# Attention's last two heads issued inside the first column group of the output projection, and the residual rows loaded behind that group

## The chip, the cores and the metric

The kernel runs on one core of a Trainium2 chip. A core has a matrix engine (PE, TensorE), a vector engine (DVE), a scalar engine (ACT), a general engine (POOL, hardly used here) and SP, which issues the transfers between device memory and the core's own memory. Each engine works through its own queue in order and waits for the others by semaphores. The metric is the time of one execution in microseconds of device time, the median of several runs.

## What is computed

A two-layer trunk on one sequence of 512 tokens with 2048 features, all in float32. Layer one is an mLSTM; layer two, which the change touches, is a chunked band attention over 16 heads of 128 features with a gate, then an output projection, a normalisation, and the residual. Cut to that:

```python
def band_attention_mixer(h, k, v, w_in, rel_table, w_out):
    Bn, S, _ = h.shape
    qz = h @ w_in
    q = qz[..., :B_WIDTH].reshape(Bn, S, B_HEADS, B_DH)
    z = qz[..., B_WIDTH:]
    o = chunk_band_attention(q, k, v, rel_table)
    y = o.reshape(Bn, S, B_WIDTH) * jax.nn.silu(z.astype(F32))
    return y.astype(h.dtype) @ w_out
...
        x = (x.astype(F32) + gate[:, None, :] * rmsnorm(y, g_post[l])).astype(x.dtype)
```

`chunk_band_attention` scales the scores of a head's queries with its keys, adds a bias by relative position, masks what lies ahead of the chunk, takes a softmax over the keys, and multiplies with the values. k and v come from one shared projection (kv_w) computed before.

## The kernel before, in words

**Precision.** Every product of float32 numbers is made of three matmuls: each operand is split into a high part (a cast on ACT, line 181) and a low part (a subtraction on DVE, line 182), and high x high, high x low and low x high are summed. All matmuls are issued from line 223 (`mm`), the transposes from line 1014.

**Weights.** They stream in as pieces of up to 128 x 1024 numbers (512 KB), in one fixed order. `wpiece` (its load is line 199) takes the next piece: it loads it into a raw buffer (`wr`), casts the high part (`wh`) and subtracts the low part (`wl`). Raw buffers rotate; every third piece can go to an own buffer in a pool named by `spare`, where one is set. Pieces are issued ahead of the work that uses them by a scheduler with priorities, as far as buffers are free. The same raw buffers take the rows `y2r` that are mentioned below.

**Attention.** For each head h, `queries(h, mid)` projects queries and gate (`proj_s`, tiles ps_dz, ps_cz, ps_az, ps_bz, four pieces of weights a head), scales the queries, takes the gate's SiLU (`sz`), splits the keys and fetches the bias (line 983). `weights(h, ...)` makes four rounds of scores (`ps_s`), adds the bias and takes the row's extreme (line 1001), exponentiates on ACT (line 1002), and normalises on DVE (lines 1003 and 1004). `flipped(h, ...)` transposes the weights (`ps_t`, ten transposes, line 1014), splits them (`pt`) and the values (`vv`). `mixed(h, ...)` multiplies them with the values (`ps_o`), multiplies with the gate on DVE (line 1032) and stores the product in device memory (`y2c`, line 1033). Keys and values of a head come from device memory by `fetch` (lines 961 and 962), three heads at a time. The steps are staggered: while head h's query projection runs, its third piece's hook (`mid`) issues `mixed(h-2)` and `weights(h-1)`, and `flipped(h-1)` follows the projection. After head 15's projection two rounds are left, without a projection beside them: `mixed(14)`, `weights(15)`, `flipped(15)`, and then `mixed(15)`.

**The last output projection.** It has four column groups of 512 columns (g). In a group, `proj_b` goes through eight pieces of weights, two blocks of 128 rows each (k0 = 0, 2, ... 14), with four sums `ps_y` open (one for each 128 tokens, m): 24 matmuls a piece, 192 a group. The left operand is read back from `y2c`, two heads at a time, by `y2_tile` (`y2r`, line 1071) and split into `y`; it is kept for the other groups. `proj_b` takes a table `at` of hooks by k0, which are called ahead of the piece. At a group's end each sum is evicted (`evac`, line 782) and squared (line 783). The fourth group is done in two halves, and the finished rows get the norm and the residual (`finish`) between and behind them. The residual rows `x2` (eight loads of 512 KB, line 1062) are issued ahead of the first group.

**Memory.** Pools are opened and closed like a stack, on a left and a right side; a new pool's tiles lie over those of closed ones and wait for their last readers. `kq` (operands of the query projection, and before the change the key and value rows), and `att` (the rest of attention) are on the left and close together at attention's end; `op` (the evicted sums) and `x2` are opened over them.

Of the kernel before, what the change touches and what calls it, by code (L numbers as in the profile page):

```python
# [9 lines left out]
F32 = mybir.dt.float32  # L10
# [5 lines left out]
P = 128  # L16
D = 2048
S = 512
KT = D // P
# [8 lines left out]
BH = 16  # L28
# [7 lines left out]
PAIRS = [(0, 1), (2, 3)]  # L36
# [96 lines left out]
def hybrid_trunk(ctx, tc, xT, xN, c, adaT, cols, wst, wg, ext, kc, out):  # L133
    nc = tc.nc
# [8 lines left out]
    def pool(name, bufs=1, **kw):  # L143
        return tc.tile_pool(name=name, bufs=bufs, reuse_waits="tile", **kw)
# [5 lines left out]
    xsc = dram.tile([4, P, D], F32, name="xsc")  # L150
# [34 lines left out]
    spare = [None]  # L185
# [58 lines left out]
    def proj_b(mat, xs, pss, ms=range(4), kts=KT, at={}, late=0):  # L244


        held = []
        for k0 in range(0, kts, 2):
            if k0 in at:
                at[k0]()  # L250
            held.append((k0, *wpiece(mat)[0]))
            if k0 >= kts - 2 * late and k0 < kts - 2:
                continue
            for group in [[pm] for pm in zip(pss, ms)] if k0 == kts - 2 else [list(zip(pss, ms))]:
                for ka, hi, lo in held:
                    for j in range(2):
                        k = ka + j
                        x = xs(k) if callable(xs) else xs[k]
                        w = slice(j * 512, (j + 1) * 512)
                        for ps, m in group:  # L260
                            t = slice(m * P, (m + 1) * P)
                            mm3(ps, x[:, 0, t], x[:, 1, t], hi[:, w], lo[:, w], k == 0, k == kts - 1)
            held.clear()
# [136 lines left out]
    for q in range(4):  # L400
        t = sp.tile([P, 4, S], F32, name=f"xt{q}")
# [8 lines left out]
    for i in range(4):  # L410
        ps = newp(f"ps_c{i}")
# [8 lines left out]
    for q in range(4):  # L420
        pair = []
# [30 lines left out]
    for k0, k1 in BLOCKS:  # L452
# [10 lines left out]
        for i, acc in enumerate(later):  # L463
            ps = newa(f"ps_l{i}_{k0}")
# [154 lines left out]
    for h in range(NH):  # L619
# [6 lines left out]
        for i in range(4):  # L626
            if h > HALF:
                if i % 2 == 0:
                    zs = pair((i // 2) * (V0 // 2) + h * DK, f"zq{h}_{i}")
                ps = zs[i % 2]  # L630
            elif h < 2:
                ps = (lead, qk1)[h][i]
            else:
                ps = newp(f"ps_qk{h}_{i}")
# [24 lines left out]
        pr, tot = [], []  # L659
        at = {8 + 2 * j: lambda j=j: scores(h, j, qk, pr, nm, nmd, tot) for j in range(4)} if h else {}  # L660
# [11 lines left out]
        for m in range(4):  # L672
            if m < 3:
                t = hp.tile([P, 2, S], F32R, tag="qk", name=f"v{h}_{m}", bufs=4)
                split(t[:, 0, :], t[:, 1, :], pv[m])
            else:
                t = hp.tile([P, S], F32, tag="v3", name=f"v{h}_{m}")
# [6 lines left out]
        for i in range(4):  # L684
            if h >= HALF:
                f = HEAD_PAIRS if h > HALF else RAMP[i]
# [5 lines left out]
            elif h:  # L692
                ps = newp(f"ps_o{h}_{i}")
# [87 lines left out]
    def evac(ps, m, g, dst):  # L781
        nc.vector.tensor_tensor(dst, ps, gb, op=ALU.mult)
        nc.scalar.activation(newa(f"sqy{m}_{g}"), ps, AF.Square, accum_out=ssq[:, 4 * m + g : 4 * m + g + 1])
# [169 lines left out]
    tst.close()  # L953


    at = ast.enter_context(pool("att"))
    kv = []

    def fetch(h):
        t = kq.tile([P, 2, S], F32, tag="kv", name=f"kv{h}", bufs=3)  # L960
        nc.sync.dma_start(t[:, 0, :], ksc[h // 2][:, h % 2, :])
        nc.sync.dma_start(t[:, 1, :], vsc[h // 4][:, h % 4, :])
        kv.append(t)
# [3 lines left out]
    def queries(h, mid):  # L967

        if h < BH - 1:
            fetch(h + 1)  # L970
        z = at.tile([P, 4, 256], F32, tag="z", name=f"z{h}", bufs=2)
        proj_s("b_w_in", h2, h2s, ATT_PAIRS, z[:, 0:2, :], z[:, 2:4, :], f"z{h}", kq, 3, {2: mid})
        qz = z.rearrange("p a t -> p (a t)")
        nc.scalar.mul(qz[:, :S], qz[:, :S], P**-0.5)
        q = at.tile([P, 2, 384], F32R, tag="q", name=f"q{h}", bufs=2)
        split(q[:, 0, :], q[:, 1, :], qz[:, P:S])
        sz = qz[:, S:]
        nc.scalar.activation(sz, sz, AF.Silu)
        k = at.tile([P, 2, S], F32R, tag="kk", name=f"k{h}")
        split(k[:, 0, :], k[:, 1, :], kv[h][:, 0, :])  # L980
        bias = at.tile([P, S], F32, tag="b", name=f"bias{h}", bufs=2)
        b0 = bsc[h]
        nc.sync.dma_start(bias, bass.AP(b0.tensor, b0.offset + P - 1, [[EXTW - 1, P], [1, S]]))
        nc.vector.memset(bias[:64, 448:512], NEG)
        return (qz[:, :P], q, k, bias), sz

    def weights(h, q0, q, k, bias):

        mx = at.tile([P, 12], F32, tag="mx", name=f"mx{h}", bufs=2)
        pr = []  # L990
        for i in range(4):
            n = P * (i + 1)
            ps = newa(f"ps_s{h}_{i}")
            if i == 0:
                mm(ps[:, :n], q0, kv[h][:, 0, :P], True, True)
            else:
                t = slice(P * (i - 1), P * i)
                mm3(ps[:, :n], q[:, 0, t], q[:, 1, t], k[:, 0, :n], k[:, 1, :n], True, True)
            s = at.tile([P, n], F32, tag=f"s{i}", name=f"s{h}_{i}")
            m, l, r = (mx[:, 3 * i + j : 3 * i + j + 1] for j in range(3))  # L1000
            nc.vector.tensor_tensor_reduce(s, ps[:, :n], bias[:, S - n :], -1.0, 3e38, ALU.add, ALU.min, m)
            nc.scalar.activation(s, s, AF.Exp, bias=m, scale=-1.0, accum_out=l)
            nc.vector.reciprocal(r, l)
            nc.vector.tensor_scalar(s, s, r, None, op0=ALU.mult)
            pr.append(s)
        return pr

    def flipped(h, pr):
        pts = []
        for j in range(4):  # L1010
            n = S - P * j
            ps = newa(f"ps_t{h}_{j}")
            for i in range(j, 4):
                nc.tensor.transpose(ps[:, P * (i - j) : P * (i - j + 1)], pr[i][:, P * j : P * (j + 1)], ident)
            if j < 3:
                t = at.tile([P, 2, n], F32R, tag=f"pt{j}", name=f"pt{h}_{j}")
                split(t[:, 0, :], t[:, 1, :], ps[:, :n])
            else:
                t = at.tile([P, n], F32, tag=f"pt{j}", name=f"pt{h}_{j}")
                nc.scalar.copy(t, ps[:, :n])  # L1020
            pts.append(t)
        v = at.tile([P, 2, 384], F32R, tag="vv", name=f"vv{h}")
        split(v[:, 0, :], v[:, 1, :], kv[h][:, 1, :384])
        return pts, v

    def mixed(h, pts, v, sz):
        ps = newa(f"ps_o{h}")
        for j in range(3):
            d = slice(P * j, P * (j + 1))
            mm3(ps[:, P * j :], v[:, 0, d], v[:, 1, d], pts[j][:, 0, :], pts[j][:, 1, :], j == 0, False)  # L1030
        mm(ps[:, 384:], kv[h][:, 1, 384:], pts[3], False, True)
        nc.vector.tensor_tensor(sz, ps, sz, op=ALU.mult)
        nc.sync.dma_start(y2c[h // 2][:, h % 2, :], sz)

    qs, ptv, szs = {}, {}, {}
    for h in range(BH + 2):
        pr = []

        def mid():
            if h > 1:  # L1040
                mixed(h - 2, *ptv.pop(h - 2), szs.pop(h - 2))
            if 0 < h <= BH:
                pr.extend(weights(h - 1, *qs.pop(h - 1)))

        if h < BH:
            qs[h], szs[h] = queries(h, mid)
        else:
            mid()
        if 0 < h <= BH:
            ptv[h - 1] = flipped(h - 1, pr)  # L1050
    ast.close()


    ost = ExitStack()
    op = ost.enter_context(pool("op", bufs=KT))
    rp = spare[0] = ost.enter_context(pool("x2", bufs=8))
    yo = [[] for _ in range(4)]
    x2 = []
    for m in range(4):
        t = [rp.tile([P, 2, S], F32, tag="x2", name=f"x2_{m}_{i}") for i in range(2)]  # L1060
        for i in range(2):
            nc.sync.dma_start(t[i], xsc[m, :, 2 * i * S : 2 * (i + 1) * S].rearrange("p (a t) -> p a t", a=2))
        x2.append([t[g // 2][:, g % 2, :] for g in range(4)])

    y2 = []

# [11 lines left out]
    def finish(m):  # L1078
        rs = row_rstd(m)
        for g in range(4):  # L1080
            y = yo[m][g]
            nc.vector.scalar_tensor_tensor(y, y, rs, x2[m][g], op0=ALU.mult, op1=ALU.add)
            nc.sync.dma_start(out[m, :, g * S : (g + 1) * S], y)

    for g in range(4):
        gate_row(1, g)
        for pair in [range(4)] if g < 3 else PAIRS:
            ps = [newp(f"ps_y1_{g}_{m}") for m in pair]
            at = {4: lambda: finish(0), 6: lambda: finish(1)} if pair == PAIRS[1] else {}
            proj_b("b_w_out", y2_tile, ps, ms=pair, at=at, late=3 if pair == PAIRS[1] else 0)  # L1090
            with tc.high_priority(AHEAD):
                for p, m in zip(ps, pair):
                    yo[m].append(op.tile([P, S], F32, tag="o", name=f"yo{m}_{g}"))
                    evac(p, m, g, yo[m][g])
    finish(2)
    finish(3)
    assert wpos[0] == len(order)
# [56 lines left out]
```

## Time and profile before

| | |
|---|---|
| median of 3 runs | 2856.14 us (2855.57 to 2857.32) |
| span of the profiled execution | 2852.6 us, from its first to its last instruction |
| the profiled execution's own time | not measured apart from its span |
| granted PE clock, mean | 0.993 |
| attention's first query projection begins on PE | 2236.45 us |
| its last one ends on PE | 2637.06 us |
| first ps_y of the last output projection | 2659.41 us |
| first eviction of its column groups 0, 1, 2 | 2709.25, 2752.77, 2796.29 us |

The page's times are microseconds from the start of the span. A row of a timeline is start, duration, engine, line, operation, out<-in and count, and in brackets the idle time before it with what ended it; consecutive equal instructions are one row. A row of the waits is engine and line, what it waited for, the total, how often, and the longest. SPq rows are issues of transfers on SP: their duration is that of the issue and not of the transfer. In a window's row, PEclk is the granted clock as a share of full speed.

### The profile page before, as it was taken

What the parts mean: (1) busy time and instruction counts of PE and PEld (TensorE: products, weight loads), DVE (VectorE), ACT (ScalarE), POOL (GpSimd) and SP (SyncE); (2) the same over time, 40 slices, a digit from 0 to 9 for tenths busy, and PEclk for the clock granted to TensorE, in tenths of its full rate; (3) what the DMA queues carried; (4) which work ended last, traced back from release to release, by engine and by line L of the source; (5) the groups of instructions that cost most, each with busy time, mean ns of one, the idle gap of its engine ahead of it and who ended that gap; (6) DMA issues with size and microseconds to landing.
All of it is one profiled execution on the core that took longest, in us unless ns stands there. A gap on an engine that the chain in (4) does not pass through costs nothing.

```text
span 2852.6 us, 40697 instructions
## 1 busy us (share of the span) xinstructions
PE 2796.1 (98%) x15308; PEld 2425.8 (85%) x15308; DVE 2074.9 (73%) x3680; ACT 1337.4 (47%) x2005; POOL 0.2 (0%) x4
## 2 busy tenths in 40 slices
PE   7999999999999999999999999999999999999798
PEld 5787888888888989989898888888998999999687
DVE  7986978778688766857766445567875899998425
ACT  4244524234234544545545445577334566666323
POOL 0000000000000000000000000000000000000000
PEclk9999999999999999999999999999999999999899
DMA  8875687878764232332325657787336433333534
GB/s 298 301 245 185 232 308 247 296 236 279 260 236 132 93 115 97 108 100 100 104 96 168 205 197 241 232 285 259 137 137 210 141 126 117 121 126 123 184 104 173
DMA packets 177117, 524.61 MB, mean 184 GB/s; under 512 B 18788, under 2 KB 36228, under 8 KB 176408
## 3 DMA queue, kind: packets, MB, share of 16 engines
q1 hardware_dynamic: 176920, 522.01, 54.1%
q8 instruction: 120, 1.97, 0.3%
q14 instruction: 77, 0.63, 0.1%
HBM read 488.33 MB, written 38.85 MB: 185 GB/s over the span
## 4 chain that ended last, share of the span: by engine, by line
PE 86%; DVE 6%; DMA 4%; ACT 2%; issue 1%; SPq 0%; DVEq 0%; ACTq 0%
PE ps_y L223 18%; PE ps_v L223 10%; PE ps_o L223 5%; PE ps_z L223 5%; PE ps_azo L223 4%; PE ps_qk L223 4%; PE ps_kv L223 4%; PE ps_bzo L223 3%; PE ps_az L223 3%; PE ps_l L223 3%; PE ps_cz L223 2%; PE ps_dz L223 2%; PE ps_czo L223 2%; PE ps_dzo L223 2%; PE ps_s L223 2%; PE ps_bz L223 2%
## 5 line engine op out<-in xcount | busy, mean ns | idle before, releaser
L181 ACT CAST wh<-wr 128x1024 fp32r<-128x1024 f32 (+3 forms) x586 | 585.1, 1000 | 860.0 <-PE ps_y L223 210.0
L182 DVE TENSOR_TENSOR wl<-wr,wh 128x1024 fp32r<-128x1024 f32 (+3 forms) x586 | 678.5, 1160 | 421.5 <-ACT wh L181 416.7
L223 PE MATMUL ps_y<-wh,y 128*128 128x512 f32 x1536 | 478.6, 392 | 10.6 <-ACT wh L181 6.0
L223 PEld LDWEIGHTS ps_y<-wh,y 128*128 128x128 f32 x1536 | 289.9, 189 | 72.1 <-ACT wh L181 6.2
L223 PE MATMUL ps_v<-wh,h 128*128 128x512 f32 x1024 | 321.6, 390 | 0.4 <-DVE cv L529 0.4
L223 PE MATMUL ps_y<-wl,y 128*128 128x512 f32 x768 | 300.6, 391 | 0.0
L181 ACT CAST wsh<-ws 128x384 fp32r<-128x384 f32 (+1 forms) x253 | 138.4, 547 | 321.5 <-issue 127.3
L223 PEld LDWEIGHTS ps_v<-wh,h 128*128 128x128 f32 x1024 | 192.3, 188 | 40.5 <-issue 1.2
L182 DVE TENSOR_TENSOR wsl<-ws,wsh 128x384 fp32r<-128x384 f32 (+1 forms) x253 | 151.5, 599 | 99.8 <-ACT wsh L181 98.3
L223 PE MATMUL ps_v<-wl,h 128*128 128x512 f32 x512 | 199.8, 390 | 0.0
L381 DVE CUSTOM_DVE_ANT_0 ada<-ada,scB,cl 128x1024 f32<-128x1024 f32 x128 | 163.7, 1280 | 25.7 <-DMA ada<-in_adaT 25.6
L381 DVE CUSTOM_DVE_ANT_0 ada<-ada,scB,mod 128x1024 f32<-128x1024 f32 x128 | 163.9, 1280 | 19.9 <-DMA ada<-in_adaT 18.4
L223 PEld LDWEIGHTS ps_y<-wl,y 128*128 128x128 f32 x768 | 145.0, 189 | 30.6 <-DVE wl L182 0.9
L223 PE MATMUL ps_kv<-wh,hkv 128*128 128x512 f32 x512 | 159.3, 391 | 0.0
L206 DVE TENSOR_TENSOR ws<-wr 128x256 f32<-128x256 f32 (+1 forms) x253 | 112.2, 451 | 34.9 <-DMA wr<-in_wst 31.8
L223 PE MATMUL ps_qk<-h,wh 128*128 128x512 f32 x384 | 119.2, 390 | 0.0
L223 PE MATMUL ps_o<-h,wh 128*128 128x512 f32 x384 | 118.2, 389 | 0.0
L223 PE MATMUL ps_z<-h,wh 128*128 128x512 f32 x384 | 118.2, 389 | 0.0
L223 PEld LDWEIGHTS ps_v<-wl,h 128*128 128x128 f32 x512 | 96.2, 188 | 19.8 <-issue 0.9
L223 PEld LDWEIGHTS ps_kv<-wh,hkv 128*128 128x128 f32 x512 | 95.7, 188 | 19.5
L223 PE MATMUL ps_l<-h,wh 128*128 128x512 f32 x320 | 99.4, 392 | 1.3 <-ACT q L467 0.5
L223 PE MATMUL ps_kv<-wl,hkv 128*128 128x512 f32 x256 | 99.9, 390 | 0.1
(385 smaller groups left out, 5916.0 us busy)
## 6 DMA issues: line engine op xcount, KB each, us to landing
wr<-in_wst SPq DMA_DIRECT2D x520, 512.0 KB, 3.7
ada<-in_adaT SPq DMA_DIRECT2D x256, 512.0 KB, 5.9
xt<-nsc SPq DMA_DIRECT2D x46, 256.0 KB, 4.3
yr<-ysc SPq DMA_DIRECT2D x16, 512.0 KB, 4.3
wr<-in_wst SPq DMA_DIRECT2D x30, 256.0 KB, 4.0
wr<-in_wst SPq DMA_DIRECT2D x16, 384.0 KB, 5.8
bsc<-in_ext SPq DMA_DIRECT2D x16, 320.0 KB, 6.2
xt<-in_xT SPq DMA_DIRECT2D x4, 1024.0 KB, 7.0
```

The costliest lines, as they stand in the source:

```text
L181: nc.scalar.copy(hi, src)
L182: nc.vector.tensor_tensor(lo, src, hi.bitcast(F32), op=ALU.subtract)
L206: nc.vector.tensor_tensor(t[:, : 2 * w], r[:, w : 3 * w], r[:, : 2 * w], op=ALU.subtract)
L223: nc.tensor.matmul(ps, a, b, start=start, stop=stop)
L381: pin(nc.vector.tensor_tensor_reduce(at, at, scB[:, j * D // 2 : (j + 1) * D // 2], 1.0, mod[:, i : i + 1] if j else col(CB + i), ALU.mult ...
```

## The change

Three things are done. First, the last two rounds of attention are no longer issued behind head 15's projection but as hooks of the first column group of the output projection: `mixed(14)` and `weights(15)` ahead of k0 = 2, `flipped(15)` ahead of k0 = 6, `mixed(15)` ahead of k0 = 8. Second, `x2` is opened, and its eight loads are issued, behind the first column group (`last_rows`); the own raw buffer of every third piece moves to the pool `op`, which is now opened over the operands of head 15's query projection. Third, since attention's tiles now have to outlive `kq`, the pool `att` goes to the right side and closes behind the first group, and the key and value rows `kv` move from `kq` to it. There they lie over tiles of the key and value projection that are on the right side.

```diff
--- before.py
+++ after.py
@@ -953,11 +953,12 @@
     tst.close()
 
 
-    at = ast.enter_context(pool("att"))
+    tail = ExitStack()
+    at = tail.enter_context(pool("att", side="right"))
     kv = []
 
     def fetch(h):
-        t = kq.tile([P, 2, S], F32, tag="kv", name=f"kv{h}", bufs=3)
+        t = at.tile([P, 2, S], F32, tag="kv", name=f"kv{h}", bufs=3)
         nc.sync.dma_start(t[:, 0, :], ksc[h // 2][:, h % 2, :])
         nc.sync.dma_start(t[:, 1, :], vsc[h // 4][:, h % 4, :])
         kv.append(t)
@@ -1033,34 +1034,41 @@
         nc.sync.dma_start(y2c[h // 2][:, h % 2, :], sz)
 
     qs, ptv, szs = {}, {}, {}
-    for h in range(BH + 2):
+    def attend(h, pr):
+        if h > 1:
+            mixed(h - 2, *ptv.pop(h - 2), szs.pop(h - 2))
+        if 0 < h <= BH:
+            pr.extend(weights(h - 1, *qs.pop(h - 1)))
+
+    for h in range(BH):
         pr = []
-
-        def mid():
-            if h > 1:
-                mixed(h - 2, *ptv.pop(h - 2), szs.pop(h - 2))
-            if 0 < h <= BH:
-                pr.extend(weights(h - 1, *qs.pop(h - 1)))
-
-        if h < BH:
-            qs[h], szs[h] = queries(h, mid)
-        else:
-            mid()
-        if 0 < h <= BH:
+        qs[h], szs[h] = queries(h, lambda: attend(h, pr))
+        if h:
             ptv[h - 1] = flipped(h - 1, pr)
     ast.close()
 
 
     ost = ExitStack()
-    op = ost.enter_context(pool("op", bufs=KT))
-    rp = spare[0] = ost.enter_context(pool("x2", bufs=8))
+    op = spare[0] = ost.enter_context(pool("op", bufs=KT))
     yo = [[] for _ in range(4)]
     x2 = []
-    for m in range(4):
-        t = [rp.tile([P, 2, S], F32, tag="x2", name=f"x2_{m}_{i}") for i in range(2)]
-        for i in range(2):
-            nc.sync.dma_start(t[i], xsc[m, :, 2 * i * S : 2 * (i + 1) * S].rearrange("p (a t) -> p a t", a=2))
-        x2.append([t[g // 2][:, g % 2, :] for g in range(4)])
+
+    def last_rows():
+
+        tail.close()
+        rp = ost.enter_context(pool("x2", bufs=8))
+        for m in range(4):
+            t = [rp.tile([P, 2, S], F32, tag="x2", name=f"x2_{m}_{i}") for i in range(2)]
+            for i in range(2):
+                nc.sync.dma_start(t[i], xsc[m, :, 2 * i * S : 2 * (i + 1) * S].rearrange("p (a t) -> p a t", a=2))
+            x2.append([t[g // 2][:, g % 2, :] for g in range(4)])
+
+    pr = []
+
+    def turn_last():
+        ptv[BH - 1] = flipped(BH - 1, pr)
+
+    ending = {2: lambda: attend(BH, pr), 6: turn_last, 8: lambda: attend(BH + 1, None)}
 
     y2 = []
 
@@ -1086,12 +1094,14 @@
         gate_row(1, g)
         for pair in [range(4)] if g < 3 else PAIRS:
             ps = [newp(f"ps_y1_{g}_{m}") for m in pair]
-            at = {4: lambda: finish(0), 6: lambda: finish(1)} if pair == PAIRS[1] else {}
-            proj_b("b_w_out", y2_tile, ps, ms=pair, at=at, late=3 if pair == PAIRS[1] else 0)
+            hooks = {4: lambda: finish(0), 6: lambda: finish(1)} if pair == PAIRS[1] else {} if g else ending
+            proj_b("b_w_out", y2_tile, ps, ms=pair, at=hooks, late=3 if pair == PAIRS[1] else 0)
             with tc.high_priority(AHEAD):
                 for p, m in zip(ps, pair):
                     yo[m].append(op.tile([P, S], F32, tag="o", name=f"yo{m}_{g}"))
                     evac(p, m, g, yo[m][g])
+        if g == 0:
+            last_rows()
     finish(2)
     finish(3)
     assert wpos[0] == len(order)
```

In the changed kernel the line numbers behind line 960 are 1 to 9 higher: the transposes are line 1015, `y2r` line 1079, the residual loads line 1063.

## The prediction

> **What bounds the kernel now.** I read the page first, for the engine that fills the span.
>
> ```profile
> span 2852.6 us, 40697 instructions
> PE 2796.1 (98%) x15308; PEld 2425.8 (85%) x15308; DVE 2074.9 (73%) x3680; ACT 1337.4 (47%) x2005; POOL 0.2 (0%) x4
> ```
>
> PE is the bound, so only a stretch in which PE stands or runs slowly can give anything back. The one that the change touches begins where the last query projection ends (2637.06) and ends with the first column group's last eviction. The busy time by windows shows it; the columns are length, busy time of PE, PEld, DVE, ACT and POOL, granted clock, DMA share and GB/s.
>
> ```profile
> 2637.06:2712.46 75.40, 60.06 (x248) 47.24 (x247) 32.11 (x55) 28.81 (x50) 0.00 (x0) 0.86 0.52 182
> 2644.18:2647.60 3.42, 1.72 (x10) 0.97 (x9) 2.78 (x11) 2.00 (x9) 0.00 (x0) 0.97 0.17 65
> 2647.60:2651.00 3.40, 1.97 (x6) 1.21 (x5) 1.49 (x3) 1.44 (x4) 0.00 (x0) 0.50 0.00 0
> ```
>
> Of 75.40 us PE is busy for 60.06, so it stands for 15.3, and its clock is 0.86 on average. The waits of PE in that stretch name what it stood for:
>
> ```profile
> PE ps_y L223 <- ACT wh L181: 6.0, 1, 6.0
> PE ps_y L223 <- ACT y L181: 4.6, 1, 4.6
> PE ps_t L1014 <- DVE pt L182: 2.5, 2, 1.4
> PE ps_t L1014 <- DVE s L1004: 1.5, 1, 1.5
> PE ps_o L223 <- ACT pt L1020: 0.4, 1, 0.4
> ```
>
> The chain of waits, with SP's timeline, says why the two large ones are there.
>
> ```profile
> 2643.26 11.27 SPq L1033 DMA_DIRECT2D y2c<-z  x2
> 2654.62 0.38 SPq L199 DMA_DIRECT2D wr<-in_wst  x1
> 2655.06 1.39 SPq L1062 DMA_DIRECT2D x<-xsc  x3
> 2661.03 1.88 SPq L1062 DMA_DIRECT2D x<-xsc  x4
> ...
> 2654.62 3.67 DMA wr<-in_wst
> 2658.31 1.05 ACT wh L181
> ...
> 2670.97 6.16 DMA y2r<-y2c
> 2677.16 0.63 ACT y L181
> ```
>
> The projection's first weight piece is issued at 2654.62, behind the stores of heads 14 and 15, then needs 3.67 us to land and 1.05 to be cast: the 6.0 wait. The third pair's rows (y2r) are issued at 2670.97, behind eight residual loads, and need 6.16: the 4.6 wait.
>
> **What the projection needs when nothing is late.** DVE's eviction of the first two columns starts once in each group:
>
> ```profile
> 2709.25 1.28 DVE L782 TENSOR_TENSOR yo<-ps_y,ssum 128x512 f32<-128x512 f32 x2
> ...
> 2752.77 1.28 DVE L782 TENSOR_TENSOR yo<-ps_y,ssum 128x512 f32<-128x512 f32 x2
> ```
>
> A group of 192 matmuls takes 2752.77 - 2709.25 = 43.52 us, 0.227 each. The attention work that also lies in the stretch is priced from PE's timeline at full clock:
>
> ```profile
> 2637.06 1.15 PE L1014 MATMUL ps_t<-kcs,s 128*128 128x128 f32 x9
> 2639.64 0.33 PE L1014 MATMUL ps_t<-kcs,s 128*128 128x128 f32 x1 [1.44 <-DVE pt L182]
> ...
> 2521.30 1.73 PE L223 MATMUL ps_o<-pt,vv 128*128 128x512 f32 x9
> 2523.09 0.39 PE L223 MATMUL ps_s<-kv,z 128*128 128x128 f32 x2
> 2523.23 0.60 PE L223 MATMUL ps_s<-k,q 128*128 128x256 f32 x3
> 2472.55 1.49 PE L223 MATMUL ps_s<-k,q 128*128 128x384 f32 x6
> ```
>
> By starts: ten transposes about 1.15, a head's ps_o 2523.09 - 2521.30 = 1.79, its scores 0.14 + 0.44 + 1.33 = 1.91. Two heads of transposes and ps_o and one of scores: 2 x 1.15 + 2 x 1.79 + 1.91 = 7.8. The floor is thus 43.5 + 7.8 = 51.3 us against 75.40: 15.3 of waits and 60.06 - 51.3 = 8.8 of slow clock (and ends of matmuls) could go.
>
> **The change part by part.** First the order on PE, from head 14's last attention products on; names carry the tile, ps_y_0_m is row block m of the first column group. Before:
>
> ```order
> L223 MATMUL ps_s_0_24775<-kv_24082,z_24423 128x128
> L223 MATMUL ps_o_24761<-pt_3_24756,kv_23741 128x128
> L223 MATMUL ps_s_1_24782<-k_24727,q_24723 128x256 x3
> L223 MATMUL ps_s_2_24791<-k_24727,q_24723 128x384 x3
> L223 MATMUL ps_s_3_24800<-k_24727,q_24723 128x512 x3
> L1014 MATMUL ps_t_0_24809<-kcs,s_0_24777 128x128
> ```
>
> Now:
>
> ```order
> L223 MATMUL ps_s_0_24822<-kv_24082,z_24423 128x128
> L223 MATMUL ps_s_1_24829<-k_24727,q_24723 128x256 x2
> L223 MATMUL ps_y_0_0_24766<-wh_24772,y_0_0_24778 128x512
> L223 MATMUL ps_y_0_1_24767<-wh_24772,y_0_0_24778 128x512
> L223 MATMUL ps_y_0_2_24768<-wh_24772,y_0_0_24778 128x512
> L223 MATMUL ps_y_0_3_24769<-wh_24772,y_0_0_24778 128x512
> L223 MATMUL ps_s_1_24829<-k_24727,q_24723 128x256
> ```
>
> The first weight piece's 24 matmuls now stand among head 15's scores; behind the scores come two more pieces (48 matmuls), then head 15's transposes, the fourth piece, head 15's ps_o, and the last 96. On SP the first piece (wr_24770) has gone ahead of both stores. Before:
>
> ```order
> L1033 DMA y2c_97<-z_24085 128x512
> L1033 DMA y2c_97<-z_24423 128x512
> L199 DMA wr_24879<-in_wst 128x1024
> L1062 DMA x_0_0_24858<-xsc 128x1024
> L1062 DMA x_0_1_24859<-xsc 128x1024
> ```
>
> Now:
>
> ```order
> L199 DMA wr_24770<-in_wst 128x1024
> L199 DMA wr_24960<-in_wst 128x1024
> L1079 DMA y2r_24900<-y2c_92 128x1024
> L1079 DMA y2r_24966<-y2c_93 128x1024
> L1034 DMA y2c_97<-z_24085 128x512
> ```
>
> All eight residual loads come behind y2r_25131, the last pair's rows.
>
> *First piece.* Its buffer now lies over the query projection's operands and is free with their last use (about 2636.1), so it is issued there and lands, by the 3.67 above, at 2639.8. ACT can cast it only behind the gate's SiLU:
>
> ```profile
> 2641.18 0.63 ACT L978 ACTIVATE z<-z 128x512 f32<-128x512 f32 x1
> 2658.31 2.94 ACT L181 CAST wh<-wr 128x1024 fp32r<-128x1024 f32 x3 [8.58 <-DMA wr<-in_wst]
> 2659.39 3.50 DVE L182 TENSOR_TENSOR wl<-wr,wh 128x1024 fp32r<-128x1024 f32 x3 [5.20 <-ACT wh L181]
> ```
>
> ACT is free at about 2641.7, so wh is there at 2642.8 and wl, 1.2 later, at 2644.0. PE reaches the first ps_y at 2642.1: a wait of 0.7, and, after four matmuls and a score, about 0.2 for wl. With the 1.4 after head 14's transposes, which stays, 2.3 to 2.5 us of the 15.3 remain.
>
> *Head 15's softmax.* Weight casts now stand on ACT ahead of its exponentials (three, 2.94 us, over by 2644.7) and among them (one more, and four of y at 0.63). The last score ends behind the first piece's other 20 matmuls, at 2644.0 + 20 x 0.227 + 1.8 = 2650.3; 0.98 + 4 x 0.63 of casts and some 1.5 of the softmax's own behind it (its wait in the table above) make the last row ready at about 2655.3. Cover: the two pieces behind the scores, 48 x 0.227 = 10.9 us, to 2661.2, so 6 us in hand. Zero, at the price of the second rival if the cover is gone. Head 15's ps_o is covered likewise by the fourth piece, 24 x 0.227 = 5.4 us, against the 1.4 + 1.0 + 0.4 that its transposes and casts wait now.
>
> *The stores and last rows.* Head 15's ps_o ends at 2661.2 + 1.15 + 5.4 + 1.8 = 2669.6. DVE's product (half of the 1.28 above, for the same size) and the store put its rows' load at about 2673 with 2 to 3 us for the store, an estimate by half of the quoted transfer; at that transfer's 6.16 they are there by 2679, cast by 2681, and PE wants them after 72 of the last 96 matmuls, 16.3 us behind ps_o (2686). Zero, with 5 us to spare.
>
> *Residual rows behind the group.* 4 MB in the 43.5 us of the second group, beside its eight pieces of 0.5 MB: 8 MB, 193 GB/s. Before, this row carried more:
>
> ```profile
> 2655.00:2670.00 15.00, 10.55 (x35) 8.08 (x36) 4.63 (x4) 4.00 (x4) 0.00 (x0) 0.68 0.92 332
> ```
>
> They are first read in the last column group. Zero; if they hold up a weight piece, at most about 1 us.
>
> *The start of attention.* Key and value rows of heads 0 to 2 now lie in another pool, whose addresses come free only with the value projection's end. Their six loads, done in before by 2172, are issued with the two bias loads, one after another, from about 2239.6. In before the same place read:
>
> ```profile
> 2239.16 0.62 ACT L181 CAST k<-kv 128x512 fp32r<-128x512 f32 x1
> 2239.59 0.89 SPq L983 DMA_DIRECT2D bias<-bsc  x2
> 2244.83 0.11 DVE L984 MEMSET bias<- 64x64 f32 x1 [0.52 <-DMA bias<-bsc]
> 2247.33 1.23 DVE L182 TENSOR_TENSOR wl<-wr,wh 128x1024 fp32r<-128x1024 f32 x1 [0.79 <-ACT wh L181]
> 2252.02 0.28 PE L223 MATMUL ps_dz<-h2s,wl 128*128 128x256 f32 x1
> ```
>
> DVE stood there for the biases until 2244.8 already, and that wl, ready at 2248.6, is read at 2252.0: 3.4 us in hand. Head 0's k is now split when its load lands, about 2244.4 (4.8 us after issue, as the second bias did), its split and vv's add 1.1 us of DVE, and the first bias, fifth of eight, is wanted before that wl. At the 332 GB/s above, five of 0.26 MB take 4 us, all eight 6.3: within what is in hand. Bounds: 0, or 2 us if the transfers share badly; I take 0.7.
>
> *The clock.* The two quoted windows show the drop: PE was busy 1.72 of 3.42 us, never idle for more than 1.5 at a time, and the next 3.4 us ran at 0.50. In the new order the stretches with waits are busy for over 1.8 of 3.4, so mostly no drop; one would cost 1.7 us. Bounds 0 and 1.7, I take 0.8. [...]
>
> *Sum.* 75.4 - (51.3 + 2.4) = 21.7, less 0.7 and 0.8: 20.2 us. The profiled span of 2852.6 would be 2832.4; the median stands 3.5 above the span (the profiled execution's own time isn't shown otherwise), and I carry the difference over: 2856.1 - 20.2 = 2836 us.
>
> **The rivals.** *First, slower: the eight loads at attention's start go one after another.* Each would then land 4.8 us behind the one before: the first bias at 2239.6 + 24 = 2263.6, the second at 2278. DVE runs in order, so the wl above ends at 2265 instead of by 2252 (13 us of PE), and the next piece's, behind the second bias, at about 2280.5, where PE, 13 late, wants it one piece of some 5 us on, at 2270 (10.5 more); two pauses of that length each bring 3.4 us at half clock (1.7 each). 13 + 10.5 + 3.4 = 26.9 lost, 20.9 gained: 2862. It decides where PE stands for over 21 us. Against it: four transfers issued within 2 us (2654.62 to 2656.4) moved at 332 GB/s, and the weights among them landed in 3.67. Chance 0.05.
>
> *Second: head 15's softmax is late.* Casts stand in its engines' queues. If its last row is ready 9 us later than worked out, PE waits 3 us before the transposes and the clock falls for one or two windows (1.7 to 3.4): gain about 14.5, 2842. [...] For it: the queue is in order and depends on y2r loads; against: 6 us in hand. Chance 0.13.
>
> *Third: attention's start costs 2 to 5 us*, as the transfers share the queues with two weight pieces: 2838 to 2841. The six loads were spread over 24 us before and now fall together. Chance 0.12.
>
> *Fourth: the change doesn't do what it says*: the first piece's buffer is still held until head 15's ps_o, as its earlier place was held. Then only the y wait and one slow window go, 4.6 + 1.7: 2850. SP's order speaks against it. Chance 0.04.
>
> **How the numbers follow.** My forecast has 0.66, and the time is its own, 2836. Range: the floor without any wait is 2856.1 - 24.1 = 2832; the second rival's 2842 and the third's lie inside 2842.5, leaving out the fourth and the first. The clock, start and softmax terms at their worst ends together reach it as well. 0.2% of the time is 5.7 us, about what a measurement here can tell from no change; all cases but the first rival are faster by more. Its 0.05 I split, 0.03 slower and 0.02 within: faster 0.95.
>
> **What would show it.** Right: the first wr of the last projection issued near 2636 and its wh cast near 2642; PE's wait for wh under 1 us and none for y; the group's first eviction near 2688 instead of 2709.25; later evictions still 43.5 apart. Wrong: a wait of PE for s or pt among the ps_y (second rival), for wl or wh between 2245 and 2270 (first, third), an interval between evictions above 44 (the residual rows).

## The result, and the profile after

The changed kernel takes 2835.93 us (median of 4, 2835.43 to 2836.37) against 2855.86 us for the kernel before (median of 4, 2852.97 to 2857.32): a ratio of 0.9931, 95% interval 0.9917 to 0.9946. Forecast were 2836.0 us. The page after, its first two lines:

```profile
span 2833.7 us, 40698 instructions
PE 2790.5 (98%) x15308; PEld 2423.1 (86%) x15308; DVE 2073.8 (73%) x3680; ACT 1337.3 (47%) x2005; POOL 0.2 (0%) x4
```

PE's busy time fell by only 5.6 us, the span by 18.9: most of the gain is standing that went. (The last group's second half took 19.1 us in this profile and 18.2 in that of before; in the profiles below it takes from 18.2 to 19.1, whatever the kernel.) The same stretch as before, from head 14's transposes to the fourth eviction of the first column group, holds the same 248 matmuls (columns as in the prediction):

```profile
2637.52:2692.60 55.08, 52.87 (x248) 43.47 (x247) 31.76 (x55) 28.34 (x50) 0.00 (x0) 1.00 0.65 218
2637.00:2655.00 18.00, 15.79 (x79) 12.85 (x78) 14.58 (x33) 14.33 (x26) 0.00 (x0) 1.00 0.54 179
```

55.08 us instead of 75.40: 13.1 us less standing (15.3 to 2.2), and 7.2 us less busy time for the same matmuls, with the clock at 1.00 instead of 0.86. All of PE's listed waits from there to the end (the one for wl stands at 2816.8, in the last group; two gaps in the stretch, 0.13 and 0.15 us, don't stand in the list):

```profile
PE ps_t L1015 <- DVE pt L182: 1.4, 1, 1.4
PE ps_s L223 <- DVE mx L1002: 0.5, 1, 0.5
PE ps_y L223 <- DVE wl L182: 0.2, 1, 0.2
```

The waits for wh (6.0) and y (4.6) are gone. The chain of waits and SP's and ACT's timelines give the reasons: the first weight piece is issued at 2636.27, the casts begin when it has landed, and the residual rows (L1063) come behind the last pair's rows.

```profile
2636.27 6.36 DMA wr<-in_wst
...
2671.98 0.33 SPq L1034 DMA_DIRECT2D y2c<-z  x1
2676.14 0.33 SPq L1079 DMA_DIRECT2D y2r<-y2c  x1
2676.52 0.43 SPq L1063 DMA_DIRECT2D x<-xsc  x1
...
2642.65 2.95 ACT L181 CAST wh<-wr 128x1024 fp32r<-128x1024 f32 x3 [0.38 <-DMA wr<-in_wst]
2680.20 1.14 ACT L181 CAST y<-y2r 128x512 fp32r<-128x512 f32 x2 [2.86 <-DMA y2r<-y2c]
```

The evictions of the first groups on DVE are still one group's 43.52 us apart:

```profile
2689.39 1.28 DVE L782 TENSOR_TENSOR yo<-ps_y,ssum 128x512 f32<-128x512 f32 x2
...
2732.91 1.28 DVE L782 TENSOR_TENSOR yo<-ps_y,ssum 128x512 f32<-128x512 f32 x2
...
2776.43 1.28 DVE L782 TENSOR_TENSOR yo<-ps_y,ssum 128x512 f32<-128x512 f32 x2
```

So the residual rows took nothing from the second and third groups. At attention's start the eight loads show on ACT and DVE:

```profile
2243.91 0.62 ACT L181 CAST k<-kv 128x512 fp32r<-128x512 f32 x1 [4.60 <-DMA kv<-ksc]
...
2248.00 0.11 DVE L985 MEMSET bias<- 64x64 f32 x1 [0.58 <-DMA bias<-bsc]
2248.20 1.23 DVE L182 TENSOR_TENSOR wl<-wr,wh 128x1024 fp32r<-128x1024 f32 x1
```

The wl that had 3.4 us in hand is 0.9 later, and PE doesn't wait for it.

### The profile page after: what moved, and what is told of

Same layout as the page of the kernel before. It is cut to its first block, busy times and chain, and to the rows that moved or that the text cites. A ratio compares the mean times of both kernels' runs of the same rounds, so it can differ in the third digit from the quotient of the medians.

```text
span 2833.7 us, 40698 instructions
## 1 busy us (share of the span) xinstructions
PE 2790.5 (98%) x15308; PEld 2423.1 (86%) x15308; DVE 2073.8 (73%) x3680; ACT 1337.3 (47%) x2005; POOL 0.2 (0%) x4
## 4 chain that ended last, share of the span: by engine, by line
PE 86%; DVE 6%; DMA 4%; ACT 2%; issue 2%; SPq 0%; DVEq 0%; ACTq 0%
PE ps_y L223 17%; PE ps_v L223 10%; PE ps_o L223 5%; PE ps_z L223 5%; PE ps_azo L223 4%; PE ps_qk L223 4%; PE ps_kv L223 4%; PE ps_az L223 3%; PE ps_bzo L223 3%; PE ps_l L223 3%; PE ps_cz L223 3%; PE ps_dz L223 2%; PE ps_bz L223 2%; PE ps_s L223 2%; PE ps_czo L223 2%; PE ps_dzo L223 2%
```

## The experiments

The theory after the result was the prediction's: the first piece comes in time, matmuls of the projection cover head 15's softmax because the hooks put them there, and the residual rows no longer stand ahead of y2r. Two rivals: the hooks' places do nothing and the memory does it all, and the three parts are not all needed. In the table, the stretch is the one above, from head 14's transposes to the fourth eviction, with the same 248 matmuls in each kernel; attention is the time from its first ps_dz to the start of its last ps_bz matmul. The ratio is to the kernel before, run again in the same set (medians of 2852.81 to 2855.86 us); a dash stands where there is no ratio because a kernel ran once.

| kernel | median us (runs) | ratio to before, interval | stretch us | PE busy in it | attention us |
|---|---|---|---|---|---|
| before | 2855.86 (4) | 1 | 75.40 | 60.06 | 400.5 |
| changed | 2835.93 (4) | 0.9931 (0.9917 to 0.9946) | 55.08 | 52.87 | 400.9 |
| e1_rows_behind | 2848.35 (6) | 0.9978 (0.9966 to 0.9991) | 68.75 | 58.01 | 399.6 |
| e2_in_a_row | 2836.2 (4) | 0.9933 (0.9916 to 0.995) | 55.30 | 52.83 | 400.9 |
| e5_kv_early | 2832.96 (1) | - | 54.61 | 52.55 | 401.7 |
| e6_no_spare | 2830.59 (1) | - | 51.60 | 51.60 | 400.9 |
| e8_two_lines | 2830.49 (4) | 0.9923 (0.9907 to 0.994) | 51.96 | 51.96 | 400.5 |
| e7_ring_only | 2841.75 (4) | 0.9956 (0.9941 to 0.9972) | 61.2 | 54.0 | 400.0 |
| e6_again | 2829.89 (4) | 0.992 (0.9905 to 0.9935) | 51.60 | 51.60 | 400.0 |
| e3_rows_sooner | 2840.63 (1) | - | 57.20 | 53.11 | 401.6 |
| e9_own_in_op | 2840.54 (4) | 0.9954 (0.9939 to 0.9969) | 63.45 | 57.52 | 398.8 |
| after_again | 2834.89 (4) | 0.994 (0.9925 to 0.9955) | 54.56 | 52.51 | 401.0 |
| e8_again | 2834.73 (4) | 0.9938 (0.9922 to 0.9955) | 51.95 | 51.95 | 398.7 |

Executions of one kernel differ by up to 9.7 us (the kernel before took 2849.17 to 2858.86 in one set). Between the profiles a good part of the difference lies ahead of attention, whose first ps_dz stands between 2234.3 and 2239.6, so a difference of 3 us is read from the stretch and not from the medians.

**The residual rows alone (on the kernel before).** The loads stand in a function that is called behind the first group; nothing else.

```diff
+        if g == 0:
+            last_rows()
```

> The kernel before with one thing changed: the residual loads are written behind the first column group; attention's last rounds stay ahead of it. Theory (two separate waits, each with its slow clock): the 4.6 us wait for y goes, because its rows are issued behind one weight piece instead of behind eight residual loads, and with it the slow 3.4 us at 2678 (1.7 us): 6.3 us faster, 2849.5. The wait for wh stays at about 6. Rival (the residual loads are what holds the first weight piece too, through the memory they lie in): 12 us or more faster, with the wait for wh under 3. Second rival (the loads only move the wait to the weights behind them): 0 to 2 us faster.

The stretch is 6.65 us shorter (the medians 5.7, in the same set), and its waits are those of before without the one for y:

```profile
PE ps_y L223 <- ACT wh L181: 6.0, 1, 6.0
PE ps_t L1014 <- DVE pt L182: 2.4, 2, 1.4
PE ps_t L1014 <- DVE s L1004: 1.5, 1, 1.5
PE ps_o L223 <- ACT pt L1020: 0.4, 1, 0.4
```

That is the theory's 6.3: 4.6 of waiting and 2.05 of busy time. By an estimate 1.7 of that busy time is the slow clock behind the wait, half of the 3.41 us that ran at 0.50 in before (2678.13 to 2681.54); the mean clock of the stretch is 0.90 against 0.86. Where the rest comes from isn't shown. The wait for wh stays whole, so the residual loads were not what held the first piece: in this kernel its buffer still lies in the pool of the residual rows.

**Attention's last rounds written in a row again (on the changed kernel).**

```diff
-    ending = {2: lambda: attend(BH, pr), 6: turn_last, 8: lambda: attend(BH + 1, None)}
+    attend(BH, pr)
+    turn_last()
+    attend(BH + 1, None)
+    ending = {}
```

> The changed kernel with attention's last rounds written ahead of the output projection again, as in the kernel before; pools, own raw buffer and residual loads stay as changed. The scheduler may then still mix the two on PE, since the memory no longer ties them. Theory A (the hooks' places make the gain, by the 10.9 us of matmuls that cover the softmax): the softmax is not covered, PE waits 4 to 6 us and the clock falls: 2842 to 2846. Theory B (the memory makes it: the first piece's buffer and the residual rows no longer lie over attention's live tiles, and the order follows by itself): within 3 us of the changed kernel, 2835 to 2839.

Theory B: 55.30 against 55.08 us in the stretch, and the same time. The mixing of the two stages was not undone by the edit. On PE, around head 15's last scores, the projection's matmuls still stand, now between the first transposes too:

```order
L223 MATMUL ps_s_3_24804<-k_24727,q_24723 128x512 x3
L1015 MATMUL ps_t_0_24813<-kcs,s_0_24781 128x128
L223 MATMUL ps_y_0_0_24855<-wh_24861,y_0_1_24870 128x512
L223 MATMUL ps_y_0_1_24856<-wh_24861,y_0_1_24870 128x512
L223 MATMUL ps_y_0_1_24856<-wl_24862,y_0_1_24870 128x512
```

So the hooks' places are not what makes the gain; with the memory free the scheduler mixes the two by itself. The 10.9 us of cover that the prediction put down to the hooks are not needed either: less does, for one wait more of 0.4 us, ahead of the last transpose.

**Key and value rows fetched early (on the changed kernel).** They get a pool of their own on the left, ahead of `kq`.

```diff
+    kvs = ExitStack()
+    kvp = kvs.enter_context(pool("kvp"))
     kq = ast.enter_context(pool("kq"))
...
-        t = at.tile([P, 2, S], F32, tag="kv", name=f"kv{h}", bufs=3)
+        t = kvp.tile([P, 2, S], F32, tag="kv", name=f"kv{h}", bufs=3)
```

> The changed kernel with key and value rows in a pool of their own whose addresses are free early, so that their first six loads stand where they stood in the kernel before. Theory (the start of attention costs 0.4 us, by late splits of head 0's k and v on DVE): the last query projection ends about 0.4 us earlier measured from attention's start, PE's wait for DVE near 2259 is 0.2 instead of 0.7; the rest is unchanged: 2835.5. Rival (the start costs nothing, the 0.5 us is scatter between runs): no difference there.

The loads are early again (issued from 2145.0 to 2169.2), but attention takes 401.7 us, 0.8 more than in the changed kernel and not 0.4 less; PE's waits for z are 1.6 us in place of 1.4. Of the 2.5 us by which the span is shorter, 2.2 come from ahead of attention. The theory of the start fell: the late loads cost nothing that this shows.

**No own raw buffer in the first group (on the changed kernel), once and again.**

```diff
-    op = spare[0] = ost.enter_context(pool("op", bufs=KT))
+    op = ost.enter_context(pool("op", bufs=KT))
...
-        rp = ost.enter_context(pool("x2", bufs=8))
+        rp = spare[0] = ost.enter_context(pool("x2", bufs=8))
```

> The changed kernel without the own raw buffer in the first column group: the first weight piece takes a buffer of the common ring, is issued earlier and its matmuls come even ahead of head 14's last products, but one piece fewer is on its way. Theory A (the own buffer's early address is what brings the first piece in time): pieces two and three come late, PE waits 2 to 5 us among the first 72 ps_y: 2838 to 2841. Theory B (any buffer will do that isn't held by attention): the first 24 matmuls fill head 14's waits of 2.1 us, 2834 to 2836, and no wait for wh or wl over 0.5.

> The changed kernel without the own raw buffer in the first column group, timed: PE without waits from the last query projection to the first eviction, 48.4 us for it instead of 51.9. Theory: 3.4 us faster than the changed kernel, 2831 to 2833, so 0.9915 to 0.992 of the kernel before measured beside it. Rival (the single time was a lucky run): 2834 to 2836.

Theory B, and faster than it said (2834 to 2836 for the first run). The first piece is loaded ahead of everything that the last heads still need, and its 24 matmuls come between head 14's transposes and its products. PE is busy through the whole stretch of both runs, at a granted clock of 1.00 (read up to 2684.82 in the first); the second:

```profile
2635.95:2687.55 51.60, 51.60 (x248) 43.12 (x247) 30.85 (x56) 27.54 (x50) 0.00 (x0) 1.00 0.68 236
```

That is 3.5 us less than in the changed kernel. The edit takes nothing away but the own buffer in the first group, which lies over the query projection's operands and so can't be filled before their last use: that buffer is what cost them.

**Two lines of the change on the kernel before, and the same again.** e1's edit, and the own buffer set only behind the first group:

```diff
-    rp = spare[0] = ost.enter_context(pool("x2", bufs=8))
+    rp = ost.enter_context(pool("x2", bufs=8))
...
         if g == 0:
             last_rows()
+            spare[0] = rp
```

> The kernel before with only two lines' worth of the change: residual loads written behind the first column group, and the own raw buffer used only from then on, so that the first weight piece takes a buffer of the common ring. Attention's last rounds are written ahead of the projection, its pool stays on the left, key and value rows stay in the operands' pool. Theory (the first piece's buffer and the residual loads carry the whole gain; where the rounds are written and on which side the pool lies don't): wait for wh under 1 and none for y, PE waits at most 4 us from the last query projection to the first eviction, 2831 to 2838. Rival (the pool's move is needed, since the sums' and residual rows' tiles over attention's tiles hold PE or the weights): the wait for wh or for a sum comes back with 4 to 6 us, 2842 to 2849.

> The kernel before with the residual loads behind the group and the first piece in the common ring, beside the changed kernel on the same chip. Theory (its three and a half us without waits between the last query projection and the first eviction are real): 2829 to 2833, 48.0 us for that stretch, below the changed kernel's lowest time. Rival (a lucky chip): within 2 us of the changed kernel.

No hooks, no pool moved, no key and value rows moved, and the stretch has no wait at all:

```profile
2636.26:2688.22 51.96, 51.96 (x248) 43.01 (x247) 30.73 (x56) 27.10 (x48) 0.00 (x0) 1.00 0.70 254
```

51.96 us, and 51.95 in the second set. In the time it is 2830.49 in one set and 2834.73 in the other, beside 2834.89 for the changed kernel there. So the second forecast, a time of 2829 to 2833 and below the changed kernel's lowest, was missed, and the time came as its rival had it. The stretch is shorter than the changed kernel's both times (51.96 and 51.95 against 55.08 and 54.56), and no profile has a wait of PE from the last query projection to the end; that the whole time is shorter is not shown. What both sets show is that a fraction of the edit does no worse than the whole.

**The ring alone (on the kernel before).** The same edit of `spare`, with the residual loads left ahead of the group.

> The kernel before with the buffer alone: the first weight piece takes a buffer of the common ring; the residual loads stay ahead of the group. Theory (two waits, each with its own cause): the 6.0 for wh goes with the slow clock behind it, a wait of 3 to 8 us for y behind eight residual loads stays, now at the fifth pair of rows: 2838 to 2845. Rival (the buffer is the cause of both): no wait for y over 1, 2831 to 2836.

Two causes, as the theory has it: no wait for wh is left, nor any in attention's last rounds, and the one for y has grown, now before the fifth pair of rows. The stretch is 14.2 us shorter than before with the buffer alone, 6.65 with the residual rows alone (e1), and 23.4 with both (e8).

```profile
PE ps_y L223 <- ACT y L181: 7.1, 1, 7.1
PE ps_y L223 <- DVE wl L182: 0.2, 1, 0.2
...
2657.22 4.41 SPq L1062 DMA_DIRECT2D x<-xsc  x8
2663.84 0.32 SPq L1071 DMA_DIRECT2D y2r<-y2c  x1
```

**Residual rows sooner (on the changed kernel).** `last_rows` as a hook at k0 = 10, ahead of the last pair's rows.

```diff
-    ending = {2: lambda: attend(BH, pr), 6: turn_last, 8: lambda: attend(BH + 1, None)}
+    ending = {2: lambda: attend(BH, pr), 6: turn_last, 8: lambda: attend(BH + 1, None), 10: last_rows}
...
-        if g == 0:
-            last_rows()
```

> The changed kernel with the eight residual loads written ahead of the sixth piece of the first group, directly behind head 15's last product, so that the last pair's rows stand behind all eight on SP. Theory (a load that PE needs soon pays for the 4 MB issued ahead of it): the last rows land 10 to 14 us after the store instead of 4 to 6, and PE waits 1 to 4 us for y: 2836 to 2840. Rival (transfers share the queues evenly and 512 KB gets through): no wait, 2834 to 2836.

```profile
2675.59 4.60 SPq L1063 DMA_DIRECT2D x<-xsc  x8
2681.29 0.32 SPq L1079 DMA_DIRECT2D y2r<-y2c  x1
...
2691.72 1.14 ACT L181 CAST y<-y2r 128x512 fp32r<-128x512 f32 x2 [11.15 <-DMA y2r<-y2c]
...
PE ps_y L223 <- ACT y L181: 2.0, 1, 2.0
```

Behind eight residual loads the rows needed 2691.72 - 2681.29 = 10.4 us, against 2680.20 - 2676.14 = 4.1 in the changed kernel, and PE waited 2.0: the theory, though the rows landed 16.5 us after their store at 2675.21, which is later than its 10 to 14 (8.2 in the changed kernel). Much of the higher single time is scatter, since attention began 3.1 us later in this run.

**Loads in time, nothing to cover the softmax (on the kernel before).** e1's edit, and the own buffer in `op`:

```diff
-    op = ost.enter_context(pool("op", bufs=KT))
-    rp = spare[0] = ost.enter_context(pool("x2", bufs=8))
+    op = spare[0] = ost.enter_context(pool("op", bufs=KT))
+    rp = ost.enter_context(pool("x2", bufs=8))
```

> The kernel before with the residual loads written behind the first column group and the own raw buffer in the sums' pool, the pools otherwise as before. The first weight piece is then issued behind head 14's store, ahead of head 15's, and PE's order has no projection matmul ahead of head 15's last product. So the loads are in time, but nothing covers head 15's softmax. Theory (cover and early load are two things; the cover is worth the waits of 1.5, 1.0 and 0.4 and one or two slow stretches of the clock at 1.7): no wait for wh or y over 1, 54 to 57 us from the last query projection to the first eviction, 2838 to 2842. Rival (the early load is all, and the softmax costs PE nothing beyond the 1.4 behind head 14's transposes): 50 to 53 us, 2834 to 2837.

```profile
2642.19 0.32 SPq L1033 DMA_DIRECT2D y2c<-z  x1
2642.60 0.38 SPq L199 DMA_DIRECT2D wr<-in_wst  x1
...
PE ps_t L1014 <- DVE pt L182: 2.6, 2, 1.4
PE ps_t L1014 <- DVE s L1004: 1.5, 1, 1.5
PE ps_y L223 <- DVE wl L182: 1.3, 2, 1.1
PE ps_o L223 <- ACT pt L1020: 0.4, 1, 0.4
...
2635.99:2699.44 63.45, 57.52 (x248) 46.25 (x247) 31.86 (x56) 28.51 (x50) 0.00 (x0) 0.92 0.63 217
2637.00:2655.00 18.00, 12.07 (x50) 8.70 (x49) 11.43 (x30) 12.29 (x25) 0.00 (x0) 0.80 0.18 61
```

With the first piece issued 12 us sooner than before, no wait for wh is left. To the first eviction it is 2696.22 - 2635.99 = 60.2 us, longer than the 54 to 57 that the theory gave, though the time fits it. The attention's own waits stay, as it said, but the clock is slow for longer: if it stood at 1.00 or 0.50, as in the traces of before and changed, a mean of 0.92 over 63.45 us is 10.2 us at 0.50, by estimate three stretches of 3.4 us and not one or two. PE's busy time is 57.52 - 51.95 = 5.6 us above that of e8. Against the changed kernel the missing cover costs 63.45 - 55.08 = 8.4 us, and more than half of it is busy time (57.52 against 52.87), at a mean clock of 0.92 against 1.00. Cover and the time of the load are not quite parted here: the piece is issued 6.6 us behind the start of head 14's transposes, in the changed kernel 1.25 ahead of it.

**The changed kernel again.**

> The changed kernel again, beside the next one: 2834 to 2837, 52 us from the last query projection to the first eviction. Every theory says the same.

As expected; it gives the scatter of the stretch, 54.56 and 55.08. Beside the kernel before in the same set, the gain is 2852.81 - 2834.89 = 17.9 us.

## Why the prediction was right, point by point

*What bounds the stretch.* Right. The two large waits had the causes that SP's timeline named, and each fell with its own cause: y with the residual rows (e1, 4.6), wh with the first piece's buffer (e7). That they are separate is shown by e1 and e7, in each of which the other stays.

*The floor of 51.3 us.* Too low by 0.3 to 0.65: without a wait the stretch takes 51.60 (e6_again) and 51.95 (e8). No work was left out of it. Of the window's 248 matmuls 192 are the group's and 53 attention's (20 transposes, 22 for ps_o, 11 for scores); three lie across its ends. In the changed kernel PE is busy for 52.87 us, another 0.9 to 1.3 more. Most of this comes, by an estimate from the rows, from its four stands: ahead of a stand a matmul counts to its end (a last transpose 0.33 us), within a row only to the next one's start (about 0.1).

*The waits that remain.* 2.4 forecast, 2.2 measured, but not the same ones: 1.4 behind head 14's transposes as said; the 0.7 for wh became 0.5 ahead of a score, where PE waits for DVE's reading of the first scores, and 0.15 ahead of the first ps_y; the 0.2 for wl didn't come, for the listed one stands in the last group; 0.13 is behind the tenth transpose. e6 and e8 show that the 1.4, which the prediction took as given, goes too when a piece is there sooner.

*The first piece, the softmax, the stores.* The issue came as said, near 2636, but the transfer took 6.36 us and not 3.67, with another weight piece issued 1.0 us ahead of it; wh was ready at 2643.7 and not 2642.8. From there on the order is the forecast one, up to 0.9 us late: the last row of the softmax ready at 2655.7 (forecast 2655.3), transposes at 2662.07 (2661.2). The last rows' load was issued at 2676.14 and not about 2673, since the store took 4.2 us and not 2 to 3; the load then took 4.1 and not 6.16, so the cast from 2680.20 fits the forecast by two misses that cancel. Wrong is what makes them: the text gave the cover to the places of the hooks, and e2 and e8 show that those do nothing.

*The clock.* Forecast 0.8 of loss, measured none: 1.00 in all of the stretch. What the prediction read from before is in the trace: in the 3.41 us ahead of the drop at 2647.41 PE was busy for 1.71, with no wait over 1.5, and behind them the clock was 0.50. In the changed kernel no 3.41 us of the stretch have PE busy for less than 1.83, and the clock stayed at 1.00; that more than 1.8 would mostly do was the author's estimate. e9, where attention's short waits stay (at most 1.5), has a mean clock of 0.80 from 2637.00 to 2655.00. e7, with one wait of 7.1 us, has 1.00 from 2637 to 2655, then 0.94 to 2675 and 0.93 to 2705.

*The start.* 0.7 forecast; attention took 400.89 instead of 400.49. Six profiles with the key and value rows in their old place lie between 398.7 and 400.5 and six with them moved between 400.0 and 401.6, so the changed layout may cost about 1 us; but e5, with early loads, has 401.7. The bunched loads are not shown to be the cause, and what is stays open.

*The sum.* 20.3 us came from the stretch, against 21.7: PE's busy time was put 1.6 too low (52.87 against 51.3), its standing 0.2 too high. The clock's 0.8 was not paid, and the start took 0.4 and not 0.7. That the forecast of 20.2 and the measured 19.9 agree to 0.3 us is luck: these misses nearly cancel, the spans of the two profiles differ by 18.9, and the later set gives 17.9.

*The rivals.* The serial loads did not come: the first bias, fifth of the eight, landed 6.2 us after its issue at 2241.8, where they wanted 2263.6. The late softmax did not come: 6.4 us in hand. The third did not come: attention took 0.4 us longer, not 2 to 5. Nor did the fourth: the first piece was issued at 2636.27. The kernel e9, whose first piece is issued behind head 14's store, comes closest to it, and its stretch is 8.4 us longer than the changed kernel's.

## What to carry to other kernels

Where a wait at a seam between two stages ends with a load, ask which memory the load writes into: a buffer laid over the stage that is ending binds the next stage to it, whatever order the code is written in. Take first the edit that unbinds it (here the choice of a buffer, and a place for loads that are needed late); interleaving may then come by itself, and the larger rebuilding may be needless. Several short waits close together can cost more than their length: in e9, whose longest was 1.5 us, 4.65 of the 8.37 us lost against the changed kernel are busy time, at a mean clock of 0.92 against 1.00.

## What the runs showed of the hardware

In before the clock was 0.50 from 2647.41 to 2664.48 and from 2678.13 to 2681.54, for 17.07 and 3.41 us, and 1.00 in the rest of the stretch. Ahead of the first drop lay 3.41 us in which PE was busy for 1.71 in several pieces, with waits of at most 1.5 us; ahead of the second, 3.41 us with 0.30. In the changed kernel the clock stayed at 1.00 where the least busy 3.41 us held 1.83. Of the 17.07 us at 0.50 in before, cut in five, PE was busy for 1.98, 2.64, 0.00, 1.61 and 3.42, and behind the last, the full one, the clock was 1.00 again. Where the borders lie isn't shown.

A load of 512 KB took 3.67 us with no other load issued shortly ahead of it (first piece, before; a store was issued 0.4 us ahead), 6.36 with one other issued 1.0 us ahead (changed), and 10.4 to its cast behind eight (e3).
